# The experts' down projection in eight slices of the model's width in place of four, with the first feed-forward's gate and up taken chunk by chunk

## The chip, the cores and the metric

One core of a Trainium2 chip runs the whole network in one launch. The number that counts is the device time of that launch in microseconds (us). Engines are named by their parts in the profile: PE is TensorE's matmuls, PEld its weight loads, DVE VectorE, ACT ScalarE, POOL GpSimd, SP SyncE (which issues the DMAs). PSUM is the matmuls' accumulator memory, SBUF the memory that all engines read.

## The reference

For 256 tokens of width 1024, in float32:

```python
def expert_choice_moe(h, w_router, w_gate, w_up, w_down):   # 16 experts, 32 tokens each
    aff = softmax(h @ w_router)                              # tokens x experts
    gate, idx = top_k(aff.T, 32)                             # each expert picks its tokens
    xin = h[idx]
    hid = silu(xin @ w_gate) * (xin @ w_up)                  # hidden width 1024
    y = (hid @ w_down) * gate[..., None]                     # back to width 1024
    return zeros_like(h).at[idx].add(y)                      # combine over experts

x = x + expert_choice_moe(rms_norm(x), ...)                  # end of the first block
h = x + 0.5 * (silu(n @ w_g) * (n @ w_u)) @ w_d              # n = rms_norm(x), d_ff 2816
```

Ahead of these lines stands the first block's mixer (dilated attention and a gated recurrence); behind them come two layers with a mixer and a second feed-forward each, and in layer two a first one again. The change touches the experts' down projection (`y` and the combine) and the first feed-forward of the first layer, the last line above.

## The kernel before

Activations lie transposed: `xt` holds x as eight chunks of 128 features by 256 tokens. Weights come from memory once, in a stream of tiles of mostly 1 MiB, [128, 2048] float32. The list `stream` fixes their order; `pump` and `fetch` (L369 to L384) issue the DMAs on SyncE in that order as slots come free: 4 raw slots, and 17 ring slots of 1 MiB (`RING`). The ring also holds `xt`, the hidden values `HT` (two), the normed chunks `norm.x` (two), the partial sums `Pt` (six) and the split pairs. `st["hold"]` is the number of ring slots that stream tiles may not take.

Two kinds of tiles are in the stream. Expert weights go to TensorE as float32 as they are, which the trace shows as two records for each matmul. The others are split (`cut`, L394 to L406) into a high part by ScalarE and a low part by VectorE, and `mm3` (L478 to L481) multiplies them in three matmuls (low by high, high by low, high by high).

The down projection of the experts goes by slices of the model's width, four of 256 columns. In a slice there are 16 y steps, each with one tile: for four experts at a time, two of the eight 128-rows of the hidden width. The four experts stand in the four column groups of TensorE (32 columns each), so that a step is 2 x 4 matmuls. After four steps ScalarE copies the accumulator `y` to SBUF, and TensorE combines it by `SC` (scatter and gate in one matrix) into `moe`. After 16 steps `x` adds `moe` to two chunks of `xt`, and `Norm.split` makes their normed high and low parts without the root of the mean, which is a factor for each token and is multiplied in later (`norm.rb2`).

So the first feed-forward's gate and up can begin before the experts are done. A unit `("u", s, j)` takes hidden chunk j of 22 and the two chunks of x of slice s: 12 matmuls into one PSUM accumulator `gu` (three buffers, tag B). Units of slice 0 are copied to `Pt` by ScalarE, those of slices 1 and 2 added to `Pt` by VectorE. `quarters()` writes the order by hand: slice 0 has y steps alone; in slices 1 to 3 the units of the slice before stand between the y steps, from the fourth step on; of slice 2 five units (`KEEP`) come behind the last y step. The same order places the gate/up tiles `gs` in the stream, two y tiles early (`EARLY`).

Behind that, `first_ffn` takes slice 3's units, ends the norm (`fin1`, `fin2`), and goes through the 22 hidden chunks: unit, `evac` (add to Pt, times norm, silu, product, high and low part), `down` three chunks behind (24 matmuls into four PSUM accumulators).

Each engine works off its own queue in order. The tile framework's scheduler chooses that order from the order of the program text, the dependences, and its own cost estimates; so units and y steps on TensorE need not stand as `quarters()` lists them.

Of the kernel before, what the change touches and what calls it, by code (L numbers as in the profile page):

```python
# [32 lines left out]
NF = 22  # L33
RING, RAW, T1, T2 = 17, 4, 10, 10
WARM = (12, 32)
KEEP, EARLY = 5, 2
# [113 lines left out]
def _prepare(i):  # L150
# [12 lines left out]
    dn = f["w_expert_down"][0].reshape(4, 4, 4, 2, 128, 4, 256)  # L163
    out["wd"] = dn.transpose(5, 0, 2, 4, 3, 1, 6).reshape(4, 4, 4, 128, 2048)
    st = [128 * j for j in range(NF)]
    for l in range(2):
        for n in ("ffn1", "ffn2"):
            ga, up = _pairs(f[n + "_gate_2"][l], st), _pairs(f[n + "_up_2"][l], st)
            both = np.stack([ga, up], axis=3)
            if (n, l) == ("ffn1", 0):  # L170
                q = both.reshape(NF, 128, 4, 2, 2, 128).transpose(2, 1, 3, 0, 4, 5)
                out["f0g"] = q[:, :, :, :20].reshape(4, 128, 2, 5, 1024).transpose(0, 3, 1, 2, 4).reshape(4, 5, 128, 2048)
                out["f0h"] = q[:, :, :, 20:].reshape(4, 128, 1024)
                out["ffn1d0"] = _rows(f["ffn1_down_2"][0])
                continue
# [63 lines left out]
def _body(tc, nc, const, ringp, work, psum, a, out):  # L239
# [66 lines left out]
    def quarters():  # L306


        for q in range(4):
            yield from (("y", 0, q, i) for i in range(4))  # L310
            yield ("sc", 0, q)
        yield ("x", 0)
        for s in range(1, 4):
            n, todo = 0, 22 if s < 3 else 22 - KEEP
            sc = None
            for k in range(16):
                yield ("y", s, k // 4, k % 4)
                while n < todo and n * 13 < (k - 2) * todo:
                    yield ("u", s - 1, n)
                    n += 1  # L320
                if sc:
                    yield sc
                sc = ("sc", s, k // 4) if k % 4 == 3 else None
            while n < todo:
                yield ("u", s - 1, n)
                n += 1
            yield sc
            yield ("x", s)
        yield from (("u", 2, j) for j in range(22 - KEEP, 22))

    order, DS, GS = [], {}, {}
    for op in quarters():
        if op[0] == "y":
            order.append(op[1:])
        elif op[0] == "u" and op[2] % 4 == 0:
            order.insert(len(order) - EARLY, ("gs", op[1], op[2] // 4))
    for o in order:
        if o[0] == "gs":
            GS[o[1:]], = add([a["f0g"][o[1], o[2]] if o[2] < 5 else a["f0h"][o[1]]], 1, 1)
# [3 lines left out]
    for j in range(22):  # L343
        if j % 4 == 0:
            GS[3, j // 4], = add([a["f0g"][3, j // 4] if j < 20 else a["f0h"][3]], 1, 1)
# [919 lines left out]
    def quarter_steps():  # L1265
# [4 lines left out]
        def unit(s, j):  # L1270
            i = GS[s, j // 4]
            n = 4 if j < 20 else 2
            ahead(i)
            wh, wl = (w[:, :512 * n].rearrange("p (c j m o) -> p c j m o", c=2, j=n, m=2) for w in parts[i])
# [9 lines left out]
        for op in quarters():  # L1284
            if op[0] == "y":
                _, s, q, i = op
                pump()
                if i == 0:
                    py[s, q] = pa("y", (128, 256))
                k = DS[s, q, i]  # L1290
                w = raw[k].rearrange("p (k g n) -> p k g n", k=2, g=4)
                for c in range(2):
                    for g in range(4):
                        e = 4 * q + g
                        h = HT[e // 8][:, e % 8].rearrange("p h j s -> p (h j) s")
                        PE.matmul(py[s, q][32 * g:32 * g + 32], lhsT=h[:, 2 * i + c], rhs=w[:, c, g],  # L1296
                                  start=i == 0 and c == 0, stop=i == 3 and c == 1, skip_group_check=True,
                                  tile_position=(0, 32 * g))
                done(k)
                if i == 3:  # L1300
                    ys[s, q] = t1("ys")
# [422 lines left out]
```

## Time and profile before

| what | us |
| --- | --- |
| median of 3 runs | 1580.06 (1580.02 to 1580.49) |
| the profiled execution | 1579.6 |
| its span, first to last instruction | 1577.8 |
| PE busy | 1436.9 (91%) |
| DVE busy | 890.6 (56%) |
| ACT busy | 660.1 (42%) |
| mean DMA rate | 254 GB/s, 400.67 MB |

In the page's forty slices of 39.4 us, the experts are where TensorE's digit falls to 6 and 7 and the DMA's stands at 9: from about 300 to 700 us. The page's chain of the work that ended last gives PE 69% and DMA 23%, of which the gate/up tiles of the experts have 16% and their down tiles (`w<-in_wd`) 6%. A row such as `L1296 PE MATMUL y<-w,hidT 128*32 128x256 f32` is line 1296, TensorE, a matmul that writes tile `y` from `w` and `hidT`, with weights of 128 rows by 32 columns and an output of 128 by 256; `[0.79 <-DMA w<-in_wd]` says that the engine was idle for 0.79 us before it until that DMA landed.

### The profile page before, as it was taken

What the parts mean: (1) busy time and instruction counts of PE and PEld (TensorE: products, weight loads), DVE (VectorE), ACT (ScalarE), POOL (GpSimd) and SP (SyncE); (2) the same over time, 40 slices, a digit from 0 to 9 for tenths busy, and PEclk for the clock granted to TensorE, in tenths of its full rate; (3) what the DMA queues carried; (4) which work ended last, traced back from release to release, by engine and by line L of the source; (5) the groups of instructions that cost most, each with busy time, mean ns of one, the idle gap of its engine ahead of it and who ended that gap; (6) DMA issues with size and microseconds to landing.
All of it is one profiled execution on the core that took longest, in us unless ns stands there. A gap on an engine that the chain in (4) does not pass through costs nothing.

```text
span 1577.8 us, 25243 instructions
## 1 busy us (share of the span) xinstructions
PE 1436.9 (91%) x10552; PEld 1121.4 (71%) x10552; DVE 890.6 (56%) x1628; ACT 660.1 (42%) x1136; POOL 6.1 (0%) x11
## 2 busy tenths in 40 slices
PE   9999986676666789899999999999999999999997
PEld 8987721101112567679999988888888899988886
DVE  7976520000000224469969877675967849877673
ACT  6445220000000341145647665464645637665452
POOL 0000000000000000000000000000000000000000
PEclk9999997766768899999999999999999999999998
DMA  7536799999999889995634635554655634636440
GB/s 297 195 131 225 307 393 421 421 421 421 421 421 421 360 344 351 402 354 184 232 128 163 241 119 220 179 191 156 217 184 187 224 117 173 242 117 221 170 161 27
DMA packets 59442, 400.67 MB, mean 254 GB/s; under 512 B 6592, under 2 KB 9792, under 8 KB 11968
## 3 DMA queue, kind: packets, MB, share of 16 engines
q1 hardware_dynamic: 59184, 398.93, 65.9%
q8 instruction: 82, 1.34, 0.3%
q14 instruction: 32, 0.26, 0.0%
q10 hardware_dynamic: 144, 0.14, 0.0%
HBM read 397.99 MB, written 1.05 MB: 253 GB/s over the span
## 4 chain that ended last, share of the span: by engine, by line
PE 69%; DMA 23%; DVE 5%; ACT 2%; issue 1%; SPq 0%; DVEq 0%; ACTq 0%
DMA w<-in_we 16%; PE gu L486 16%; PE gu L487 8%; PE dn L486 8%; DMA w<-in_wd 6%; PE dn L487 4%; PE gu L479 3%; PE gu L480 2%; PE gu L481 2%; PE y L1296 2%; PE acc L480 2%; PE acc L479 1%; PE acc L481 1%; DVE wl L403 1%; PE dn L479 1%; PE dn L481 1%
## 5 line engine op out<-in xcount | busy, mean ns | idle before, releaser
L403 DVE TENSOR_TENSOR wl<-w,wh 128x1024 fp32r<-128x1024 f32 (+1 forms) x369 | 435.5, 1204 | 92.0 <-ACT wh L402 84.3
L402 ACT ACTIVATE wh<-w 128x1024 fp32r<-128x1024 f32 (+1 forms) x369 | 364.6, 1037 | 47.5 <-PE dn L486 14.9
L486 PE MATMUL gu<-xs,wh 128*128 128x512 f32 x1056 | 371.7, 395 | 0.0
L487 PE MATMUL gu<-xs,wl 128*128 128x256 f32 x1056 | 294.7, 279 | 0.0
L1233 PE MATMUL gu<-w,xin 128*32 128x512 f32 x1024 | 182.3, 806 | 67.8 <-DMA w<-in_we 67.5
L486 PEld LDWEIGHTS gu<-xs,wh 128*128 128x128 f32 x1056 | 197.9, 188 | 45.9
L487 PEld LDWEIGHTS gu<-xs,wl 128*128 128x128 f32 x1056 | 199.2, 189 | 0.2
L486 PE MATMUL dn<-hx,wh 128*128 128x512 f32 x528 | 186.6, 394 | 0.0
L1233 PEld LDWEIGHTS gu<-w,xin 128*32 128x32 f32 x1024 | 26.1, 123 | 199.6 <-DMA w<-in_we 177.8
L1239 DVE TENSOR_TENSOR hid<-sg,gu 64x512 f32<-64x512 f32 x16 | 11.0, 690 | 249.3 <-ACT sg L1238 249.3
L487 PE MATMUL dn<-hx,wl 128*128 128x256 f32 x528 | 147.5, 279 | 0.0
L486 PEld LDWEIGHTS dn<-hx,wh 128*128 128x128 f32 x528 | 99.0, 187 | 23.2
L1296 PE MATMUL y<-w,hidT 128*32 128x256 f32 x1024 | 79.6, 417 | 35.7 <-DMA w<-in_wd 35.7
L479 PE MATMUL gu<-xs,wl 128*128 128x256 f32 x352 | 103.7, 297 | 0.3 <-DVE wl L403 0.3
L481 PE MATMUL gu<-xs,wh 128*128 128x256 f32 x352 | 100.7, 287 | 0.0
L480 PE MATMUL gu<-xs,wh 128*128 128x256 f32 x352 | 100.7, 287 | 0.0
L487 PEld LDWEIGHTS dn<-hx,wl 128*128 128x128 f32 x528 | 99.6, 189 | 0.0
L1238 ACT ACTIVATE sg<-gu 64x512 f32<-64x512 f32 x16 | 9.4, 590 | 209.8 <-PE gu L1233 209.8
L1394 ACT ACTIVATE fl<-gu 128x256 f32<-128x256 f32 x132 | 49.4, 377 | 95.7 <-PE gu L487 95.4
L1395 DVE TENSOR_TENSOR fz<-gu,fl 128x256 f32<-128x256 f32 x132 | 55.2, 419 | 57.3 <-ACT fl L1394 57.1
L1296 PEld LDWEIGHTS y<-w,hidT 128*32 128x32 f32 x1024 | 31.5, 117 | 73.4 <-DMA w<-in_wd 43.9
L479 PEld LDWEIGHTS gu<-xs,wl 128*128 128x128 f32 x352 | 68.5, 196 | 13.2 <-issue 7.7
(397 smaller groups left out, 2489.4 us busy)
## 6 DMA issues: line engine op xcount, KB each, us to landing
w<-in_we SPq DMA_DIRECT2D x128, 1024.0 KB, 19.8
w<-in_wd SPq DMA_DIRECT2D x64, 1024.0 KB, 12.8
w<-in_ffn2gu SPq DMA_DIRECT2D x44, 1024.0 KB, 5.0
w<-in_ffn1d SPq DMA_DIRECT2D x22, 1024.0 KB, 5.3
w<-in_wm SPq DMA_DIRECT2D x22, 1024.0 KB, 4.9
w<-in_ffn2d SPq DMA_DIRECT2D x22, 1024.0 KB, 5.4
w<-in_ffn1gu SPq DMA_DIRECT2D x22, 1024.0 KB, 5.0
w<-in_f0g SPq DMA_DIRECT2D x20, 1024.0 KB, 7.3
```

The costliest lines, as they stand in the source:

```text
L402: hi = S.activation(wh, raw[i][:, a0:a1], AF.Copy)
L403: lo = V.tensor_tensor(wl, raw[i][:, a0:a1], wh.bitcast(F32), op=OP.subtract)
L479: PE.matmul(ps, lhsT=wl, rhs=x[:, 1], start=first, stop=False, skip_group_check=True)
L480: PE.matmul(ps, lhsT=wh, rhs=x[:, 0], start=False, stop=False, skip_group_check=True)
L481: PE.matmul(ps, lhsT=wh, rhs=x[:, 1], start=False, stop=last, skip_group_check=True)
L486: PE.matmul(ps, lhsT=wh, rhs=x, start=first, stop=False, skip_group_check=True)
L487: PE.matmul(ps[:, 0], lhsT=wl, rhs=x[:, 1], start=False, stop=last, skip_group_check=True)
L1233: PE.matmul(pg[32 * g:32 * g + 32], lhsT=xin[k // 4][:, k % 4, 32 * e:32 * e + 32], rhs=w[:, g], start=k == 0, stop=k == 7, skip_group_che ...
L1239: i = V.tensor_tensor(hid, sg, pg[64:128], op=OP.mult)
L1296: PE.matmul(py[s, q][32 * g:32 * g + 32], lhsT=h[:, 2 * i + c], rhs=w[:, c, g], start=i == 0 and c == 0, stop=i == 3 and c == 1, skip_grou ...
L1394: S.activation(zl[:, m], p[m][:, 0], AF.Copy)
L1395: V.tensor_tensor(z[:, m], p[m][:, 1], zl[:, m], op=OP.add)
```

## The change

The down projection goes by eight slices of 128 columns. A slice has eight y steps; a step's tile, again 1 MiB, holds four of the eight 128-rows for four experts, so that a step is 4 x 4 matmuls over 128 columns. Two steps fill an accumulator `y` (128 x 128), which is copied and combined as before, in one matmul of 128 columns by 256 tokens. After eight steps one chunk of `xt` is complete and normed.

A unit takes one chunk of x: six matmuls. There are eight times 22 of them. The units of chunk c stand between the y steps of slice c + 1, spread evenly by `8 * n < NF * (8 * c - 8 + k + 1 - LAG)`, without the gaps at the head of a slice. Gate/up tiles hold eight units (two tiles and one of six units, 0.75 MiB, for each chunk). `hold` falls to 6 after the first slice, where it was 7. Behind the last y step, the last chunk's units are added to `Pt` at once (`gate_up`), `evac` comes two chunks behind the unit and loses the add, and `down` follows six chunks behind the unit.

```diff
-KEEP, EARLY = 5, 2
+LAG, EARLY = 2, 2
...
+    def slices():
+        units = [("u", c, j) for c in range(7) for j in range(NF)]
+        n, sc = 0, None
+        for c in range(8):
+            for k in range(8):
+                yield ("y", c, k // 2, k % 2)
                 if sc:
                     yield sc
+                    if sc[2] == 3:
+                        yield ("x", sc[1])
+                sc = ("sc", c, k // 2) if k % 2 else None
+                while n < len(units) and 8 * n < NF * (8 * c - 8 + k + 1 - LAG):
+                    yield units[n]
+                    n += 1
+        yield sc
+        yield ("x", 7)
+        yield from units[n:]
...
             p = pb("gu")
             for m in range(2):
-                for c in range(2):
-                    mm3(p[:, m], wh[:, c, j % 4, m], wl[:, c, j % 4, m], norm.x[2 * s + c], m == 0 and c == 0,
-                        m == 1 and c == 1)
-            if j % 4 == n - 1:
+                mm3(p[:, m], wh[:, j % 8, m], wl[:, j % 8, m], norm.x[c], m == 0, m == 1)
+            if j % 8 == n - 1:
                 done(i)
...
-                w = raw[k].rearrange("p (k g n) -> p k g n", k=2, g=4)
-                for c in range(2):
+                w = raw[k].rearrange("p (k g n) -> p k g n", k=4, g=4)
+                for c in range(4):
                     for g in range(4):
...
-                    macc[s] = pa("moe")
-                y = ys.pop((s, q))
-                for m in range(2):
-                    PE.matmul(macc[s][:, m], lhsT=y[:, 128 * m:128 * m + 128], rhs=SC[q // 2][:, q % 2],
-                              start=q == 0 and m == 0, stop=q == 3 and m == 1, skip_group_check=True)
+                    macc[s] = pa("moe", (128, 256))
+                PE.matmul(macc[s], lhsT=ys.pop((s, q)), rhs=SC[q // 2][:, q % 2],
+                          start=q == 0, stop=q == 3, skip_group_check=True)
...
-                if s == 0:
-                    st["hold"], st["la"], st["late"] = 7, 1, 0
+                V.tensor_tensor(xt[:, c], macc[c], xt[:, c], op=OP.add)
+                norm.chunk(c)
+                if c == 0:
+                    st["hold"], st["la"], st["late"] = 6, 1, 0
...
+        def gate_up(j):
+            z = Pt[j // 4][:, j % 4]
+            V.tensor_tensor(z, unit(7, j), z, op=OP.add)
+
         def evac(j):
             z = Pt[j // 4][:, j % 4]
-            V.tensor_tensor(z, ps.pop(j), z, op=OP.add)
...
-        for j in range(3):
-            ps[j] = unit(3, j)
+        for j in range(6):
+            gate_up(j)
             if j == 0:
                 norm.fin1(pa)
         norm.fin2()
-        for j in range(3):
+        for j in range(4):
             evac(j)
-        for j in range(3, NF):
-            ps[j] = unit(3, j)
-            evac(j)
-            down(j - 3)
+        for j in range(6, NF):
+            evac(j - 2)
+            gate_up(j)
+            down(j - 6)
         norm.free()
         st["hold"], st["la"], st["late"] = 2, LA[1], LATE[1]
-        for j in range(NF - 3, NF):
+        for j in range(NF - 6, NF):
+            if j < NF - 4:
+                evac(j + 4)
             down(j)
```

The weights are laid out on the host to match (`wd` as 8 x 4 x 2 tiles, `f0g` as 8 x 2, `f0h` as 8).

## Rows read from the trace of the kernel before

**Rows 1.** The windows view (us, busy per engine, granted clock, DMA): three stages.

```profile
473.50:528.00 54.50, 32.85 (x337) 13.66 (x336) 2.53 (x6) 5.32 (x12) 0.00 (x0) 0.81 1.01 420
528.00:704.00 176.00, 158.57 (x1473) 121.18 (x1474) 70.06 (x87) 52.61 (x79) 0.00 (x0) 0.95 0.91 359
704.00:808.00 104.00, 104.00 (x874) 103.69 (x873) 94.73 (x156) 57.47 (x93) 0.21 (x1) 1.00 0.61 213
```

**Rows 2.** The timeline (start us, us, what): first slice's y steps on TensorE.

```profile
511.73 1.07 PE L1296 MATMUL y<-w,hidT 128*32 128x256 f32 x16 [1.41 <-DMA w<-in_wd]
...
529.20 1.03 PE L1296 MATMUL y<-w,hidT 128*32 128x256 f32 x2 [3.12 <-DMA w<-in_wd]
```

**Rows 3.** Timeline of TensorE: one y step, the last y step, the last combine.

```profile
637.49 1.05 PE L1296 MATMUL y<-w,hidT 128*32 128x256 f32 x10 [0.79 <-DMA w<-in_wd]
638.47 0.38 PE L479 MATMUL gu<-xs,wl 128*128 128x256 f32 x1
...
702.38 1.07 PE L1296 MATMUL y<-w,hidT 128*32 128x256 f32 x16
...
704.91 1.03 PE L1309 MATMUL moe<-scat,ys 128*128 128x256 f32 x4
705.59 0.47 PE L479 MATMUL gu<-xs,wl 128*128 128x256 f32 x1
```

**Rows 4.** Waits of SyncE's DMA queue (us, times, longest), 473 to 704 us.

```profile
SPq L374 <- PE y L1296: 83.5, 24, 7.4
```

**Rows 5.** Chain of waits, 570 to 600 us.

```profile
586.84 6.99 DMA w<-in_wd
```

**Rows 6.** Timeline of TensorE: first matmuls of gate/up and down, tail's steady part and end.

```profile
739.45 0.29 PE L479 MATMUL gu<-xs,wl 128*128 128x256 f32 x1
...
740.89 0.28 PE L479 MATMUL dn<-hx,wl 128*128 128x256 f32 x1
...
743.72 0.29 PE L479 MATMUL gu<-xs,wl 128*128 128x256 f32 x1
...
807.75 0.29 PE L479 MATMUL lx<-xs,wl 128*128 128x256 f32 x1
```

**Rows 7.** The page's groups (busy, mean ns | idle before): the y matmuls.

```profile
L1296 PE MATMUL y<-w,hidT 128*32 128x256 f32 x1024 | 79.6, 417 | 35.7 <-DMA w<-in_wd 35.7
```

**Rows 8.** Lines by form: the 128-column float32 matmul.

```profile
L438 PE MATMUL junk<-x,cst 128*128 128x128 f32 x64 | 7.7, 277 | 0.0
```

**Rows 9.** Timeline of TensorE: 128x32 weights over 32 columns.

```profile
52.91 0.71 PE L821 MATMUL lev<-AL,AR 128*32 128x32 f32 x62
53.56 0.39 PE L479 MATMUL aqk<-xs,wl 128*128 128x256 f32 x1
```

**Rows 10.** Timeline of VectorE in the tail.

```profile
741.77 0.68 DVE L1346 TENSOR_TENSOR Pt<-gu,Pt 128x512 f32<-128x512 f32 x1
742.37 0.42 DVE L516 TENSOR_TENSOR hx<-fh,hx 128x256 fp32r<-128x256 f32 x1
...
743.30 2.35 DVE L403 TENSOR_TENSOR wl<-w,wh 128x1024 fp32r<-128x1024 f32 x2
745.57 0.42 DVE L1350 TENSOR_TENSOR fh<-fs,Pt 128x256 f32<-128x256 f32 x1
```

**Rows 11.** Chain of waits, 704 to 726 us.

```profile
724.60 0.47 PE dn L479 x4
```

**Rows 12.** Waits, 528 to 704 us (us, times, longest).

```profile
DVE wl L403 <- ACT wh L402: 59.0, 12, 10.9
...
PEld gu L479 <- DVE wl L403: 2.6, 6, 0.8
...
PEld gu L479 <- DVE Pt L1334: 1.6, 4, 0.4
```

More of the change, by code (lines that the diff above doesn't have):

```diff
@@ L162, in _prepare @@
     out["we"] = gu
[L163 to L164 removed]
+    dn = f["w_expert_down"][0].reshape(4, 4, 2, 4, 128, 8, 128)
+    out["wd"] = dn.transpose(5, 0, 2, 4, 3, 1, 6).reshape(8, 4, 2, 128, 2048)
     st = [128 * j for j in range(NF)]
@@ L302, in _body, with add_gs @@
     GU, DN, WM, WO = {}, {}, {}, {}
[L306 to L320, printed above, removed]
+    def slices():
[4 more added lines that the diff above has]
+                yield ("y", c, k // 2, k % 2)
                 if sc:
                     yield sc
[L323 to L329, printed above, removed]
+                    if sc[2] == 3:
[7 more added lines that the diff above has]
+        yield from units[n:]
     order, DS, GS = [], {}, {}
-    for op in quarters():
+    for op in slices():
         if op[0] == "y":
             order.append(op[1:])
-        elif op[0] == "u" and op[2] % 4 == 0:
-            order.insert(len(order) - EARLY, ("gs", op[1], op[2] // 4))
+        elif op[0] == "u" and op[2] % 8 == 0:
+            order.insert(len(order) - EARLY, ("gs", op[1], op[2] // 8))
+    def add_gs(c, g):
+        GS[c, g], = add([a["f0g"][c, g] if g < 2 else a["f0h"][c]], 1, 1)
     for o in order:
         if o[0] == "gs":
-            GS[o[1:]], = add([a["f0g"][o[1], o[2]] if o[2] < 5 else a["f0h"][o[1]]], 1, 1)
+            add_gs(*o[1:])
         else:
@@ L342, in _body @@
     d0 = []
-    for j in range(22):
-        if j % 4 == 0:
-            GS[3, j // 4], = add([a["f0g"][3, j // 4] if j < 20 else a["f0h"][3]], 1, 1)
+    for j in range(NF):
+        if j % 8 == 0:
+            add_gs(7, j // 8)
         if j >= 3 and (j - 3) % 2 == 0:
@@ L1262, in _body, with slice_steps, unit @@
     rfree(2)
-    def quarter_steps():
+    def slice_steps():
         norm, Pt, py, ys, macc = None, [], {}, {}, {}
-        def unit(s, j):
-            i = GS[s, j // 4]
-            n = 4 if j < 20 else 2
+        def unit(c, j):
+            i = GS[c, j // 8]
+            n = 8 if j < 16 else 6
             ahead(i)
-            wh, wl = (w[:, :512 * n].rearrange("p (c j m o) -> p c j m o", c=2, j=n, m=2) for w in parts[i])
+            wh, wl = (w[:, :256 * n].rearrange("p (j m o) -> p j m o", j=n, m=2) for w in parts[i])
             p = pb("gu")
             for m in range(2):
-                for c in range(2):
-                    mm3(p[:, m], wh[:, c, j % 4, m], wl[:, c, j % 4, m], norm.x[2 * s + c], m == 0 and c == 0,
-                        m == 1 and c == 1)
-            if j % 4 == n - 1:
+                mm3(p[:, m], wh[:, j % 8, m], wl[:, j % 8, m], norm.x[c], m == 0, m == 1)
+            if j % 8 == n - 1:
                 done(i)
             return p
-        for op in quarters():
+        for op in slices():
             if op[0] == "y":
@@ L1295, in quarter_steps @@
                         h = HT[e // 8][:, e % 8].rearrange("p h j s -> p (h j) s")
-                        PE.matmul(py[s, q][32 * g:32 * g + 32], lhsT=h[:, 2 * i + c], rhs=w[:, c, g],
-                                  start=i == 0 and c == 0, stop=i == 3 and c == 1, skip_group_check=True,
+                        PE.matmul(py[s, q][32 * g:32 * g + 32], lhsT=h[:, 4 * i + c], rhs=w[:, c, g],
+                                  start=i == 0 and c == 0, stop=i == 1 and c == 3, skip_group_check=True,
                                   tile_position=(0, 32 * g))
                 done(k)
-                if i == 3:
-                    ys[s, q] = t1("ys")
+                if i == 1:
+                    ys[s, q] = t1("ys")[:, :128]
                     S.activation(ys[s, q], py.pop((s, q)), AF.Copy)
@@ L1338, in first_ffn @@
         st["hold"] = 5
-        norm, Pt, unit = quarter_steps()
+        norm, Pt, unit = slice_steps()
         warm(AF.Silu)
         st["hold"], st["la"], st["late"] = 1, LA[0], LATE[0]
-        ps, hs, acc = {}, {}, []
+        hs, acc = {}, []
+        def gate_up(j):
+            z = Pt[j // 4][:, j % 4]
+            V.tensor_tensor(z, unit(7, j), z, op=OP.add)
         def evac(j):
             z = Pt[j // 4][:, j % 4]
-            V.tensor_tensor(z, ps.pop(j), z, op=OP.add)
             V.tensor_tensor(z, z, norm.rb2, op=OP.mult)
```

24 lines of the change are left out of this document (9 added, 15 removed).

## The prediction

> **What bounds the kernel now.** I read the windows view first. It cuts the touched stretch into three stages [rows 1]: from the first y step to 528 us the transfers are full (420 GB/s, share 1.01) and TensorE waits; from 528 to 704 us both are nearly full and neither wholly (TensorE busy 158.6 of 176, 359 GB/s); from 704 to 808 us TensorE never pauses and VectorE is busy 94.7 of 104. Everything behind 808 us is untouched code, so I let the rest of the span follow the end of this stretch one for one.
>
> 1 MiB at 420 GB/s takes 2.50 us, the unit of all sums below. The timeline shows the first stage at that pace: the sixteenth y step, last of slice 0, starts at 511.7, just after its tile has landed [rows 2]. Back from there by 15 tiles, the tile of the first step has its place in the pace at 511.7 - 37.5 = 474.2. The first gate/up matmul comes only behind 529.2, after two y records of slice 1's fifth step [rows 2]. Until then TensorE has next to nothing to do; a y step is 0.98 us (637.49 to 638.47 [rows 3]).
>
> In the second stage a transfer-only clock would bring the last y tile after 63 y tiles and 16 MiB of gate/up weights: 474.2 + 79 x 2.50 = 671.7. It ran at 702.4 [rows 3]. So 30.7 us were lost over 48 steps, 0.64 us a step. The waits view says how: SyncE's queue stood 83.5 us for slots that a y step had yet to free [rows 4]; then the chain shows the bill, a y tile issued at 586.8 when a slot came free and 7 us in flight while TensorE had nothing left [rows 5]. TensorE bunches gate/up units, tiles that have landed hold their slots meanwhile, the transfers pause, and then TensorE pauses.
>
> In the third stage a unit of gate/up takes 1.44 us and one chunk of the first down projection 2.83 (starts at 739.45, 740.89 and 743.72 [rows 6]). 27 units and 22 downs make 38.9 + 62.3 = 101.2 of the 104.4 us between the end of the last y step (702.38 + 0.98) and the next phase's first matmul at 807.75 [rows 3, 6].
>
> **The change part by part.**
>
> *Slice 0 is half as long.* The first slice is 8 tiles, and chunk 0's units start behind the eleventh y step (LAG of 2). That tile has one gate/up tile ahead of it, so it lands at 474.2 + 11 x 2.50 = 501.7, and units may start at about 502.7 in place of 530. This is the gain: 27 us of TensorE time that is idle now.
>
> *The y steps.* 64 tiles of 1 MiB as before, but each is 16 matmuls over 128 columns in place of 8 over 256; y records go from 1024 [rows 7] to 2048. The array time is equal if the four column groups still run side by side: a group of four records is 0.86/4 = 0.22 us now (0.98 less the start) and should take 0.11 with half the columns. A plain 128-column float32 record costs 7.7/64 = 0.12 us [rows 8], and the trace has a burst with 32-column weights that issues 62 records in 0.65 us, 0.0105 each [rows 9]; four of these are 0.04, well under 0.11, so issue and weight loads hide. I take 0.98 us a step. From the other side, if nothing overlapped, 32 x 0.12 = 3.84 us a step; the burst is the nearer row, being the same tiling.
>
> A rule of the Trainium skill speaks against this. Its page TensorE: Matmul & The Clock Gate, section Back-to-back issue gap, gives about 81 ns per matmul for a sustained stream of load and matmul pairs at 128 columns. By it a step would be an estimated 32 x 0.081 = 2.6 us. The burst of rows 9 at 0.0105 us disagrees with a floor of that size for column-tiled records, so I do not use it for the sum.
>
> *Gate/up units.* 176 half-units of six matmuls, 0.72 us each; the total on TensorE is unchanged. A step of slices 1 to 7 carries 22/8 = 2.75 of them: 1.98 us, with y 0.98 and the combine (32 matmuls as before; four take 705.59 - 704.91 = 0.68 us by records, two records per quarter now, 0.17 a step) 3.13 us. The transfers per step are 1 + 2.75/8 = 1.344 MiB: 3.36 us. SyncE issues the same number (88) and the same bytes.
>
> *The two clocks to the last y step.* Transfers: 63 y tiles and seven chunks of 2.75 MiB: 474.2 + 82.25 x 2.50 = 679.8. TensorE: 502.7 + 53 x 3.13 = 668.6. Transfers end last, by 11, so the two are about as close as in the kernel before and the coupling decides what is lost. The loss per step is bounded by 0 (no bunching) and 0.64 (as now, 36 us over 56 steps). Three things differ: the three unit-free steps at the head of each slice are gone, a unit is half as long, and the slots held back fall from 7 to 6, so of the 17 ring slots six rather than five are left for tiles and split pairs beside the four raw ones. A bunch is still up to one gate/up tile (8 half-units, 5.8 us, as 4 units were). I take 0.38 a step, 21 us: the last y step starts at 701.
>
> *VectorE.* Each half-unit behind chunk 0 is added to Pt separately: 154 adds in place of 66, 88 more at 0.60 us (741.77 to 742.37 [rows 10]), 53 us. About 127 fall into the y stage, whose VectorE is busy 70 of 176 now [rows 1]: per step 2.75 x 0.60 + 0.344 x 2.27 for the splits (two cuts, 743.30 to 745.57 [rows 10]) + 0.15 for the norm = 2.6 of 3.36 us. It fits, so I cost it at nothing there; its cover is that slack, and without it a stall of three accumulators follows (rival below). ScalarE's copies of y are twice as many over half the columns, and 22 Pt copies stay. GpSimd's queue is not touched.
>
> *The tail.* Left behind the last y step are 5 half-units of chunk 6 and 22 of chunk 7, 27 x 0.72 = 19.4 us, and the downs, 62.3: with the norm's small matmuls 84. The first down waits for the whole norm; now it starts at 724.6 [rows 11], 19 us behind the combine, and these 19 us are just what the 27 half-units cover, because their adds no longer stand behind the norm. VectorE: what it does in 704 to 808 now (94.7) less the splits of 2.75 MiB (6.2) is 88.5. Tail between 84 and 92; I take 88, VectorE's number, against 104.4.
>
> Sum: 701 + 1 + 88 = 790 against 807.75, 18 us less. The profiled execution took 1579.6 (span 1577.8), 0.5 under the median of 1580.06; the forecast is on the median: **1562 us**.
>
> **The rivals.**
>
> A. *As forecast*, 1562 (1552 to 1571 with the tail's bounds and a loss of 0.25 to 0.5 a step). Chance 0.48.
>
> B. *The bunching stays.* If slots, not unit size, make the loss, it is 0.64 a step again: the last y step at 716, end 805, 3 us less: 1577 (1573 to 1581). For it: SyncE's 83.5 us of waits for y [rows 4]. Against: one slot more and evener units. Chance 0.17.
>
> C. *Even spreading removes nearly all of it*: 8 us lost, tail 84: end 773, 35 less: 1545. For it: TensorE still has 0.23 us a step to spare. Against: no stretch of the second stage shows it. Chance 0.15.
>
> D. *Slower: VectorE stops TensorE through the three gate/up accumulators.* VectorE works in order, and now stands 59.0 us in 12 waits at the head of a split for ScalarE's half, 4.9 us each; TensorE lost only 2.6 + 1.6 us by it [rows 12], since three accumulators were 4.3 us of work. With half-units, two free ones cover 1.44. A wait of 4.9 and the add behind it (0.6) then cost 5.5 - 1.44 = 4.1. If 10 of the 24 gate/up tiles catch it, TensorE's clock gains 41, less the 12 it has to spare over 53 steps: 29 late, end at 819: 1591. It decides from about seven tiles (7 x 4.1 - 12 = 17). Against: the waits now are mostly VectorE idling with nothing else to do. Chance 0.15.
>
> E. *The column groups stop overlapping*: 3.84 a step, TensorE needs 5.99 a step, the last y step at 820, 1680. Against: [rows 9]. Chance 0.05.
>
> By the skill's 81 ns, E would give an estimated 502.7 + 53 x 4.74 + 88 = 842, about 1614.
>
> **How the numbers follow.** 0.2% (3.2 us) is about what a measurement can tell from no change. A and C are faster, as is half of B: 0.48 + 0.15 + 0.09 = 0.72; the other half of B is no change: 0.08; D and E slower: 0.20. The range 1541 to 1584 holds A, B and nearly all of C, and leaves out E and most of D, with C's far end about 0.2. The likeliest case's own range is 1552 to 1571.
>
> **What would show it.** The first gate/up matmul at about 503 us; y records 2048, with a step of 32 near 1.0 us; last y step near 701, with SyncE's waits for y well under 83 us; 154 adds into Pt with hardly any TensorE wait for VectorE before the last y step; the next phase's first matmul near 790, VectorE full in the tail. It is wrong if a y step takes over 1.4 us, if TensorE's waits for Pt adds exceed 15 us (D), or if the last y step stays behind 710 (B).

## The result, and the profile after

The changed kernel takes **1591.59 us** (1590.80 to 1593.75 in 4 runs) where the one before takes 1580.28 beside it: a ratio of 1.0072, 95% interval 1.0055 to 1.0089. It is slower by 11 us (the profiled executions' spans are 1589.8 and 1577.8). The forecast was 1562, 30 us less, with a range that ends at 1584.

The windows view of the changed kernel, cut where the first gate/up matmul, the last y step and the next phase begin, answers to [rows 1]. The columns are the same: length, busy time of TensorE, its weight loads, VectorE, ScalarE and GpSimd, granted clock, DMA share, GB/s.

```profile
473.50:516.60 43.10, 27.46 (x476) 19.26 (x476) 2.14 (x5) 5.03 (x12) 0.00 (x0) 0.76 1.01 420
516.60:724.70 208.10, 187.19 (x2514) 161.13 (x2514) 135.47 (x185) 60.46 (x100) 0.00 (x0) 0.98 0.88 340
724.70:820.00 95.30, 89.10 (x729) 87.71 (x718) 88.47 (x148) 50.01 (x86) 0.00 (x0) 0.95 0.57 203
```

The first stage is 13.5 us shorter than before (gate/up began at 530.2), the second 35 longer (173 before, from that matmul to the last y step), the third 9 shorter (104.4 before). Net, the next phase starts 12.2 us later. In the middle stage the transfers run at 340 GB/s, below before's 359, while TensorE still pauses for 21 us: neither is full.

The start, on ScalarE's timeline of the changed kernel (start, length, what; the bracket is the idle time ahead):

```profile
494.32 0.42 ACT L545 ACTIVATE ss<-x 128x256 f32<-128x256 f32 x1 [1.25 <-DVE x L1310]
501.11 0.28 ACT L1299 ACTIVATE ys<-y 128x128 f32<-128x128 f32 x1 [6.38 <-PE y L1293]
508.57 0.28 ACT L1299 ACTIVATE ys<-y 128x128 f32<-128x128 f32 x1 [7.18 <-PE y L1293]
513.75 0.28 ACT L1299 ACTIVATE ys<-y 128x128 f32<-128x128 f32 x1 [4.91 <-PE y L1293]
513.93 0.50 ACT L532 ACTIVATE xs<-x,vec 128x256 fp32r<-128x256 f32 x1
514.33 1.99 ACT L401 ACTIVATE wh<-w 128x1024 fp32r<-128x1024 f32 x2
```

Chunk 0 of x is summed by 494.3 and its first gate/up tile has landed at 496.6, but the normed chunk (`xs`) and the tile's high part (`wh`) stand in ScalarE's queue behind three copies of y, each of which waits 5 to 7 us for its y steps. ScalarE is idle nearly all of these 19 us. The first gate/up matmul starts at 516.68.

The middle, in the chain of waits of the changed kernel (start, length, what), the place where a gate/up tile begins:

```profile
583.04 1.05 PE y L1293 x32
584.14 0.15 issue
584.29 1.06 ACT wh L401
585.37 1.24 DVE wl L402
586.60 0.14 issue
586.74 0.36 PE gu L478
```

The copy of y between them is on ScalarE's timeline:

```profile
584.11 0.28 ACT L1299 ACTIVATE ys<-y 128x128 f32<-128x128 f32 x1 [6.15 <-PE y L1293]
584.29 1.99 ACT L401 ACTIVATE wh<-w 128x1024 fp32r<-128x1024 f32 x2
```

A y step ends, ScalarE copies it, then splits the next gate/up tile, then VectorE makes the low part, and only then TensorE goes on with that tile. The transfer is not what is late: this tile had landed at 565.9, 18 us before its split began, and each of the first twenty gate/up tiles of the stage lay for 10 to 18 us. The waits view counts what TensorE lost, over 473 to 720 us (us, times, longest):

```profile
PE gu L478 <- DVE wl L402: 18.4, 16, 2.9
PE y L1293 <- DMA w<-in_wd: 13.6, 11, 3.8
PEld gu L478 <- DVE Pt L1325: 3.4, 17, 0.2
...
SPq L373 <- PE y L1293: 100.0, 27, 9.1
SPq L373 <- DVE wl L402: 81.1, 19, 13.7
```

Sixteen waits of a matmul for a low part, where before there were two, 0.3 us in all (weight loads had the 2.6 of [rows 12]). SyncE's queue waits longer for y steps than in [rows 4], and longer for splits (a raw slot comes free when its tile is split; 64.3 before).

The end of the stretch, on TensorE's timeline of the changed kernel, answers to [rows 3, 6, 11]:

```profile
723.86 1.08 PE L1293 MATMUL y<-w,hidT 128*32 128x128 f32 x32
...
739.91 0.69 PE L569 MATMUL rbT<-cst,rt 128*128 128x128 f32 x2 [2.06 <-DVE rt L473]
743.87 1.01 PE L478 MATMUL dn<-hx,wl 128*128 128x256 f32 x3 [3.28 <-ACT hx L514]
...
819.97 0.29 PE L478 MATMUL lx<-xs,wl 128*128 128x256 f32 x1
```

The y matmuls on the page, against [rows 7]:

```profile
L1293 PE MATMUL y<-w,hidT 128*32 128x128 f32 x2048 | 79.3, 292 | 13.6 <-DMA w<-in_wd 13.6
```

Twice the records, half the columns, the same busy time (79.6 before). A step's 32 records take 1.08 us, 0.034 each. For these records, with 32-column weights in four column groups, the trace disagrees with the 81 ns that the Trainium skill (TensorE: Matmul & The Clock Gate, section Back-to-back issue gap) gives for each matmul in a stream of load and matmul pairs at 128 columns.

### The profile page after: what moved, and what is told of

It is laid out like the page before. It is cut to its first block, busy times and chain, and to the rows that moved or that the text cites. A ratio compares the mean times of both kernels' runs of the same rounds, so it can differ in the third digit from the quotient of the medians.

```text
span 1589.8 us, 27418 instructions
## 1 busy us (share of the span) xinstructions
PE 1445.0 (91%) x11576; PEld 1150.3 (72%) x11576; DVE 949.6 (60%) x1716; ACT 660.6 (42%) x1152; POOL 6.1 (0%) x11
## 4 chain that ended last, share of the span: by engine, by line
PE 70%; DMA 18%; DVE 8%; ACT 3%; issue 1%; DVEq 0%; SPq 0%; ACTq 0%
PE gu L485 15%; DMA w<-in_we 15%; PE gu L486 8%; PE dn L485 8%; PE dn L486 4%; PE y L1293 3%; DVE wl L402 3%; PE gu L478 3%; DMA w<-in_wd 3%; PE gu L479 2%; PE gu L480 2%; ACT wh L401 2%; PE acc L479 2%; PE acc L478 1%; PE acc L480 1%; PE gu L1232 1%
## 5 line engine op out<-in xcount | busy, mean ns | idle before, releaser
L401 ACT ACTIVATE wh<-w 128x1024 fp32r<-128x1024 f32 (+2 forms) x369 | 364.7, 1037 | 26.2 <-PE dn L485 14.9
L478 PE MATMUL gu<-xs,wl 128*128 128x256 f32 x352 | 107.1, 304 | 18.6 <-DVE wl L402 18.4
L485 PEld LDWEIGHTS dn<-hx,wh 128*128 128x128 f32 x528 | 99.0, 188 | 23.1
L1325 DVE TENSOR_TENSOR Pt<-gu,Pt 128x512 f32<-128x512 f32 x132 | 89.9, 690 | 41.1 <-PE gu L480 39.5
L1293 PE MATMUL y<-w,hidT 128*32 128x128 f32 x2048 | 79.3, 292 | 13.6 <-DMA w<-in_wd 13.6
L1390 ACT ACTIVATE fl<-gu 128x256 f32<-128x256 f32 x132 | 49.4, 376 | 95.7 <-PE gu L486 95.4
```

The costliest lines, as they stand in the source:

```text
L401: hi = S.activation(wh, raw[i][:, a0:a1], AF.Copy)
L478: PE.matmul(ps, lhsT=wl, rhs=x[:, 1], start=first, stop=False, skip_group_check=True)
L485: PE.matmul(ps, lhsT=wh, rhs=x, start=first, stop=False, skip_group_check=True)
L1293: PE.matmul(py[s, q][32 * g:32 * g + 32], lhsT=h[:, 4 * i + c], rhs=w[:, c, g], start=i == 0 and c == 0, stop=i == 1 and c == 3, skip_grou ...
L1325: V.tensor_tensor(Pt[j // 4][:, j % 4], p, Pt[j // 4][:, j % 4], op=OP.add)
L1390: S.activation(zl[:, m], p[m][:, 0], AF.Copy)
```

## The experiments

All are edits of the changed kernel, so the yardstick is 1591.59; ratios are to the kernel before. Times of stages are from each run's own trace: "first unit" is the first gate/up matmul (after: 516.7), "last y" the start of the last y record (724.7), "end" the next phase's first matmul (820.0). Behind it all traces have the same 769.8 to 771.0 us.

**Which part costs: the split's place, the adds, the half-units, the slices.** e_split2 fetches each gate/up tile one y step earlier and splits it two earlier.

```diff
-LAG, EARLY = 2, 2
+LAG, EARLY, SOON = 2, 3, 2
...
+            elif op[0] == "u" and op[2] % 8 == 0:
+                cuts.setdefault(max(ny - SOON, 0), []).append(GS[op[1], op[2] // 8])
...
                 pump()
+                for k in cuts.get(ny, []):
+                    split(k)
```

> The changed kernel with each gate/up tile's split put two y steps ahead of the tile's first unit in the program (and the tile itself one y tile earlier in the stream); nothing is computed more or less. Theory S (the split is asked for only when its first unit is due, its ScalarE half stands behind a y copy and its VectorE half behind Pt adds, and TensorE stands at the first unit: about 4 of each slice's 32 us): TensorE's waits for the split nearly go, a slice takes 28 to 29 us, the last y step comes at 695 to 705 in place of 724, about 1570 us. Theory V (VectorE's 88 more adds set the pace): its work is the same, so 1588 to 1593. Theory P (TensorE's own time grew, by twice as many changes between y and units): 1588 to 1593.

1584.40, ratio 1.0026 (1.0016 to 1.0036): 7 us off. TensorE's waits for the low part fall from 18.4 to 10.3, last y 715.3, where theory S wanted 695 to 705. The late split costs, but it is not all.

e_noadd leaves the adds of chunks 1 to 6 out.

```diff
-                else:
+                elif c == 6 and j >= 17:
                     V.tensor_tensor(Pt[j // 4][:, j % 4], p, Pt[j // 4][:, j % 4], op=OP.add)
```

> The changed kernel without the adds into Pt of chunks 1 to 6 ahead of the last y step (it leaves these parts of gate and up out of the sum). Theory V: VectorE loses about 76 us of work in the y stage, so the stage shrinks by 20 us or more, to about 1570 us. Theory S: the VectorE half of a split no longer stands behind adds, but its ScalarE half still stands behind the y copy and the split is still asked for late: 3 to 10 us, 1581 to 1588. Theory P: no change in the y stage, 1589 to 1593.

1586.53, ratio 1.0038 (1.0027 to 1.0050): with VectorE's work in the middle stage cut from 135 to 53 us, only 5 us come off, and 14.8 us of TensorE's waits for low parts stay. The adds are the smaller part of it.

e_pairs keeps the eight slices and takes units of two chunks, as before; e_single keeps four slices and takes units of one chunk.

```diff
-        units = [("u", c, j) for c in range(7) for j in range(NF)]
+        units = [("u", s, j) for s in range(3) for j in range(NF)]      # e_pairs
...
-            for k in range(8):
-                yield ("y", c, k // 2, k % 2)
+            for k in range(16):                                         # e_single
+                yield ("y", c, k // 4, k % 4)
```

> One part alone: the down projection in eight slices of 128 columns, but gate/up units of two chunks (12 matmuls, 66 adds) as before the change, which can begin only behind the second slice. If the 128-column y steps cost time by themselves: above 1585 us. If the halved units do (S, V and P all say so): within 5 us of the kernel before, 1577 to 1584.

> The other part alone: the down projection in four slices of 256 columns as before, but gate/up units of one chunk, spread evenly, and the changed tail; units begin only behind the first slice of 16 y steps. S, V and P: the stage pays for the halved units without the earlier start: 1592 to 1605 us. If the halved units were free: 1575 to 1582.

e_pairs 1586.73, ratio 1.0037 (1.0023 to 1.0050); e_single 1608.38, ratio 1.0169 (1.0147 to 1.0191). Their first units start at 530.6 and 532.3, as before. Neither isolates one part: both spread the units evenly, and e_single has the changed tail too. By its own bounds e_pairs (above 1585) speaks for y steps that cost something. Its trace does not show that: a y record occupies 0.0335 us there (a step 1.07), but TensorE waits 12.4 us for low parts, which the kernel before hardly does (0.3). e_single loses otherwise than the changed kernel: of its 28 us over the kernel before, 18 lie between the first unit and the last y record (190.9 against 172.9), with 21 us of waits for y tiles, and 8 behind it (112.9 against 104.7). That the whole change costs less than e_single goes with its early start; no run shows that it is the only reason.

**The start.** x_norm takes the two ring slots of the normed chunks at the start of the stage, by a one-column write, so that `xs` need not wait for y tiles to leave them. x_pre0 does that, and takes two pairs of parts (used in turn by all gate/up tiles up to chunk 6) and the six slots of `Pt` ahead as well. x_pre2 is x_pre0 with e_split2's earlier fetch and split; x_pre2t adds to x_pre2 that the last chunk's adds come behind the norm's root.

```diff
-        norm, Pt, py, ys, macc = None, [], {}, {}, {}
+        norm, Pt, py, ys, macc = Norm(vc("ffn1n", 0, 8)), [], {}, {}, {}
+        for h in norm.x.half:
+            V.tensor_copy(h[:, 0, 0, 0:1], xt[:, 0, 0:1])
...
+        pairs, turn = [tuple(ralloc([128, 2048], F32R, n) for n in ("wh", "wl")) for _ in range(2)], [0]   # x_pre0, x_pre2
...
-LAG, EARLY = 2, 2
+LAG, EARLY, SOON = 2, 3, 2                    # x_pre2 (x_pre0: 2, 2, 0)
...
+            if j:
+                behind(add, st["gate"])       # x_pre2t
```

> The changed kernel with the two ring slots of the normed chunks taken ahead of the first y step (by a one-column write), where they were taken when the first slice was done. Theory R (slots: transfers that stand further down the program take every ring slot as it comes free, so the normed chunks, the split pairs and Pt get theirs only when a y step frees one, and their ScalarE halves stand behind that step's copy): chunk 0's high part comes at 494 in place of 513.9, but the first split pair still has to wait for a slot, so the first gate/up matmul moves only from 516.7 to 507 to 513, and the total to 1582 to 1590 us. Rival S (only the place of the split in the program): the first gate/up matmul at about 503, the rest as in the changed kernel, 1577 to 1581 us.

> The changed kernel with all that the stage keeps taken from the ring ahead of the first units: the normed chunks, two split pairs that are used in turn, and the six Pt tiles; two ring slots and the four raw ones are left for tiles. The split stands where it stood in the program. Theory R: first gate/up matmul at 502 to 507, few waits for splits, last y step at 695 to 705 (724 in the changed kernel), 1565 to 1575 us. Rival S: only the start gets better; the waits inside the slices stay, 1577 to 1585 us. Rival Q (fewer tiles in flight starve TensorE of y tiles): 1590 us or more.

> As the run with all kept slots taken ahead, and each split asked for two y steps before its first unit. R alone: within 3 us of that run, either way. S beside R: 3 to 12 us better than it, 1558 to 1570 us.

> As the run before it, and in the tail the adds of the last chunk's units and the splits further ahead stand behind the root of the mean on VectorE, which in the changed kernel took 6.4 us for eight small operations with an add between any two of them, while TensorE stood 6 us until the first down. If that order costs the tail its 6 to 7 us over the forecast of 88: 4 to 7 us better than the run before it. If the tail is bound by VectorE's sum of work: within 2 us of it.

x_norm: 1593.41, ratio 1.0078 (1.0061 to 1.0095), nothing gained. Its ScalarE timeline:

```profile
495.41 0.51 ACT L532 ACTIVATE xs<-x,vec 128x256 fp32r<-128x256 f32 x1 [1.25 <-DVE x L1310]
...
513.85 0.28 ACT L1301 ACTIVATE ys<-y 128x128 f32<-128x128 f32 x1 [4.74 <-PE y L1295]
514.02 2.00 ACT L401 ACTIVATE wh<-w 128x1024 fp32r<-128x1024 f32 x2
```

`xs` moved by 18.5 us, `wh` by 0.3: the split's own slots hold it there, and first unit stays at 517.4.

x_pre0: 1579.32, ratio 0.9991 (0.9981 to 1.0002). First unit at 499.3, 17 us earlier; the end moves by 13, because the middle stage became 5 longer: though it has its own pairs of parts, TensorE still waits 23.1 us for low parts (473 to 720 us). x_pre2: 1611.29, ratio 1.0197 (1.0182 to 1.0212), and x_pre2t 1613.18, ratio 1.0206 (1.0191 to 1.0221). The same early start, and then a middle stage of 244 us. TensorE's waits in x_pre2, 498 to 742 us:

```profile
PE gu L479 <- DVE wl L402: 35.1, 19, 3.7
```

Of the 17 ring slots two are left for tiles in flight there, with the four raw ones six in all. At one such wait the gate/up tile lands at 602.3, ScalarE begins its high part at 603.06, and TensorE stands from 601.85 to 605.50: the tile itself is late. I read it so that slots help at the start, where they are missing, and cost later, where tiles in flight lack them. x_pre2t says that the adds ahead of the root are not what the tail waits for: its tail is no shorter than x_pre2's (98.3 us against 97.9).

**Bunching, and the tail.** x_bunch puts all the units of a gate/up tile behind one y step, the opposite of the change's even spread. x_bunchpre is x_bunch with x_pre0's slots. a_norb leaves out the multiplication by the norm's factor for all hidden chunks but the first, 12.6 us of VectorE in the tail. x_bpool is x_bunchpre with half of that multiplication on GpSimd.

```diff
-                    yield units[n]
-                    n += 1
+                    m = min(8, NF - n % NF)               # x_bunch, x_bunchpre, x_bpool
+                    yield from units[n:n + m]
+                    n += m
...
-            V.tensor_tensor(z, z, norm.rb2, op=OP.mult)
+            if j == 0:                                    # a_norb
+                V.tensor_tensor(z, z, norm.rb2, op=OP.mult)
...
+            V.tensor_tensor(z[:, 0], z[:, 0], norm.rb, op=OP.mult)    # x_bpool
+            G.tensor_tensor(z[:, 1], z[:, 1], norm.rb, op=OP.mult)
```

> The changed kernel with the units of a whole gate/up tile (8, 8 and 6) behind one y step each, where two or three stood behind every y step; so there are three changes from y to units in a slice, not seven or eight, and all 154 units come ahead of the last y step (5 more, 3.5 us). Theory P (TensorE's own time grew: 135 ns for a gate/up record and 0.56 us for a combine, against 119 ns within a run, by the changes between kinds): gate/up records fall to 122 to 128 ns, the stage by 6 to 12 us, total 1578 to 1586 us. Theory R (slots alone): the splits still wait for a slot, 1588 to 1594 us.

> The bunched units together with all kept slots taken ahead. If P and R are two costs that add: 8 to 14 us better than the run with the slots alone (1579.3), 1565 to 1572 us, faster than the kernel before. If the one took the place of the other: 1576 to 1582 us.

> The changed kernel without the factor of the norm on hidden chunks 1 to 21 in the tail (it leaves that factor out; chunk 0 keeps it, so that the downs still wait for the root). VectorE loses 21 x 0.60 = 12.6 us of work behind the root. If VectorE's sum of work bounds the tail: 6 to 12 us less, 1579 to 1586 us. If the root's chain or TensorE bounds it: within 3 us of 1591.

> The bunched units with all kept slots taken ahead, and in the tail the up half of that factor on GpSimd, which is idle, in place of VectorE (22 x 0.27 us off VectorE). If VectorE bounds the tail and GpSimd keeps pace: 3 to 6 us better than without, 1560 to 1569 us. If GpSimd's instruction takes over 2 us or slows VectorE: no better or worse.

x_bunch: 1583.16, ratio 1.0013 (1.0001 to 1.0025), 8 us off the changed kernel. Its waits of TensorE, 517 to 718 us:

```profile
PE y L1294 <- DMA w<-in_wd: 9.5, 12, 1.8
...
PE gu L479 <- DVE wl L403: 0.9, 4, 0.3
```

The waits for low parts are gone: while TensorE does a bunch, the next split has time. In their place y steps wait 9.5 us for their tiles (1.0 in the changed kernel from its first unit on), so TensorE's pauses fall from 20.8 to 15.5 only; the other 3 us of the stage are TensorE's own time (184.0 against 187.2). With the changed kernel's slots, even spreading, which the forecast took for a gain, was a loss of 8; v_first and v_firstb below show that this does not hold with other slots. x_bunchpre, 1583.29 (1.0014; 1.0001 to 1.0026): the early start adds nothing to that, since the slots taken ahead bring the waits for low parts back (20.6 us).

a_norb: 1591.94, ratio 1.0071 (1.0054 to 1.0087). Its tail:

```profile
729.60:822.80 93.20, 87.83 (x727) 86.67 (x718) 76.67 (x127) 49.51 (x86) 0.00 (x0) 0.96 0.59 206
```

VectorE 12 us freer, the tail 2 us shorter: it is not VectorE's sum that bounds it. x_bpool, 1586.11 (1.0038; 1.0023 to 1.0053), is 3 us above x_bunchpre, but it did not relieve VectorE. VectorE's multiplication of one half took 0.81 us beside GpSimd's 0.95 for the other, where that of both halves took 0.685 in x_bunchpre; VectorE's busy time in the tail rose from 85.1 to 90.0 us. So this run says nothing on what the tail waits for.

**Do the two costs add?** v_first takes ahead only what the first unit needs: the normed chunks' slots and one pair of parts for the first tile, which then goes back to the ring; the two slots are held free from the eleventh expert on. v_firstb adds the bunching, v_firstbs a split one y step earlier to that, v_bs has those two without the slots.

```diff
-        parts[i] = (ralloc([128, 2048], F32R, f"wh{i}"), ralloc([128, 2048], F32R, f"wl{i}"))
+        parts[i] = st.pop("pair", None) or (ralloc([128, 2048], F32R, f"wh{i}"), ralloc([128, 2048], F32R, f"wl{i}"))
...
+        if e == 11:
+            st["hold"] += 2
...
+        pair = tuple(ralloc([128, 2048], F32R, n) for n in ("wh", "wl"))
+        for w in pair:
+            V.tensor_copy(w[:, 0:1], xt[:, 0, 0:1])
+        st["pair"] = pair
```

> The changed kernel, with only the slots of the normed chunks and of one pair of high and low parts taken ahead, at the eleventh expert (x_pre0 took two pairs and the four slots of Pt as well). Start theory (the first gate/up matmul waits for slots, and nothing that is taken for it is missed later): that matmul at 500 to 505 us, last y step 710 to 714, total 1577 to 1582. Rival (what x_pre0 gained came from its two alternating pairs of parts, not from the early start): the matmul early all the same, but the last y step at 718 to 724 and a total of 1584 to 1591.

> v_first, and the eight units of a gate/up tile together behind one y step, as in x_bunch. If the two costs add (start 12 to 17 us, units together 8): last y step at 700 to 706, total 1568 to 1575, below the kernel before. Rival (both draw on the same slots, and an early start only makes the later tiles wait): total 1580 to 1585, as x_bunch and x_bunchpre.

> v_firstb, and each tile is split one y step earlier (e_split2 did that to the changed kernel and took 7 us off). Split theory (TensorE still stands for the parts at a tile's first unit): 2 to 5 us below v_firstb, and the waits of gate/up matmuls for the low part below 8 us. Rival (after putting the units together no split wait on the path is left, and the earlier split only holds a pair of slots longer): within 2 us of v_firstb or up to 6 us above it.

> The changed kernel with the units together and the split one y step earlier, and no slots taken ahead. Start theory: the first gate/up matmul stays at 515 to 520, and the total at 1577 to 1582, above v_firstbs by 8 to 15 us. Rival (the start is worth nothing once the stage's pace is better, since y steps wait for the transfers): within 3 us of v_firstbs.

v_first: **1569.46** (1568.45 to 1571.13), ratio 0.9931 (0.9914 to 0.9947), faster than both kernels. v_firstb 1584.32 (1.0032; 1.0017 to 1.0046), v_firstbs 1583.06 (1.0021; 1.0006 to 1.0036), v_bs 1582.29 (1.0017; 1.0005 to 1.0029): with the units together the early start is worth nothing, so these two do not add. More than that: with v_first's slots, putting the units together costs 15 us, where it gained 8 with the changed kernel's. v_first is over 7 us better than its start theory allowed, and the start alone does not explain it: the first unit comes 17.2 us earlier, the last y record 20.6 (704.1), the end 20.5. Its waits for low parts are 3.0 us.

**Which slots.** v_pair is v_first with the pair alone taken ahead, and not the normed chunks. It also leaves `hold` at 5 when the stage begins, which v_first lowers to 1 for its four slots, so fewer ring slots are open to tiles in its first slice. v_firsts is v_first with e_split2's edit.

```diff
-        norm, Pt, py, ys, macc = Norm(vc("ffn1n", 0, 8)), [], {}, {}, {}
-        for h in norm.x.half:
-            V.tensor_copy(h[:, 0, 0, 0:1], xt[:, 0, 0:1])
+        norm, Pt, py, ys, macc = None, [], {}, {}, {}             # v_pair
...
-LAG, EARLY = 2, 2
+LAG, EARLY, SOON = 2, 3, 2                                        # v_firsts
```

> v_first without the normed chunks' slots: only one pair of high and low parts is taken ahead. x_norm showed the chunks' slots alone to give nothing (first gate/up matmul at 517.4, total 1593). Theory that both are needed: the normed chunk waits behind the evictions as in the changed kernel, the first gate/up matmul stays at 513 to 518, and the total at 1585 to 1592. Rival (the pair does all of it): the matmul at 500 to 505 and the total within 3 us of v_first's 1569.

> v_first, and each gate/up tile fetched one and split two y steps earlier, as e_split2 did to the changed kernel for 7 us. If the split's lateness is gone in v_first (gate/up matmuls wait 3.0 us for the low part in it): within 2 us of 1569, or up to 8 us above it because the parts hold their slots longer and y tiles land later. Rival (some lateness is left at each tile's first unit): 1563 to 1567.

v_pair: **1571.06** (1568.62 to 1577.42), ratio 0.9950 (0.9932 to 0.9967). With one pair of slots taken ahead, 20.5 of the 30 us that were missing are back: in the traces the first unit comes 8.3 us earlier and the middle stage is 13.4 shorter (194.7 against 208.1). The total is as the rival said, the first unit between the two. Its windows, its ScalarE at the start and in one slice, and its waits of TensorE and SyncE, 473 to 703 us:

```profile
475.00:508.30 33.30, 19.77 (x390) 14.05 (x388) 3.27 (x4) 4.58 (x10) 0.00 (x0) 0.85 1.01 420
508.30:703.00 194.70, 181.07 (x2596) 158.41 (x2598) 132.57 (x183) 60.57 (x101) 0.00 (x0) 1.00 0.95 376
703.00:798.40 95.40, 88.70 (x728) 87.55 (x721) 88.34 (x149) 51.05 (x86) 0.00 (x0) 0.96 0.61 219
```

```profile
497.36 2.00 ACT L401 ACTIVATE wh<-w 128x1024 fp32r<-128x1024 f32 x2 [1.92 <-DMA w<-in_f0g]
501.80 0.28 ACT L1306 ACTIVATE ys<-y 128x128 f32<-128x128 f32 x1 [2.44 <-PE y L1300]
501.97 0.50 ACT L532 ACTIVATE xs<-x,vec 128x256 fp32r<-128x256 f32 x1
...
577.51 3.46 ACT L401 ACTIVATE wh<-w 128x1024 fp32r<-128x1024 f32 x4
```

```profile
PE gu L478 <- DVE wl L402: 3.3, 6, 0.7
...
SPq L373 <- PE y L1300: 82.1, 28, 5.2
...
SPq L373 <- DVE wl L402: 37.6, 14, 9.1
```

The first split follows its tile's landing (497.36) in place of the third copy of y, and the first unit starts at 508.4, behind a y step whose tile landed at 507.4. The transfers of the first stage run at 420 GB/s all the same. And in the slices ScalarE splits two tiles in one go (577.51, four halves), one of them ahead of its need. That leaves 3.3 us of waits for low parts, halves SyncE's wait for splits, and gives 376 GB/s. A slice takes 29.2 us (577.4 to 606.6), where the changed kernel takes 32.0 (584.1 to 616.1). v_firsts, 1582.60 (1.0010; 0.9997 to 1.0022), has the early start as well (498.2) but 14.9 us of waits for low parts: asking for the split earlier still undoes what v_first gained.

## Why the prediction was wrong

By the traces, the 30.0 us between the end forecast (790) and the one measured (819.97) are 14.0 at the start, 8.9 in the middle and 7.1 in the tail.

**The step that failed first: "units may start at about 502.7".** It asked only for the tile and the chunk, and both were there by 497. It left out that `xs`, `wh` and `wl` each need a ring slot that y tiles held, and that on an engine that works in order a split which waits for a slot is put behind copies that wait for y. Shown: x_norm frees `xs` and nothing moves; v_pair frees the pair and the first unit comes at 508.4, v_first frees both and it comes at 499.5. This step accounts for 14.0 of the 30 us.

**The sizes on TensorE: 3.13 us a step.** From the starts of consecutive records between the first unit and the last y step (waits taken off), a gate/up matmul occupies 0.135 us, a y step 1.11 and a combining record 0.281, against 0.12, 0.98 and 0.17: 25 us more in all (118.5 + 55.1 + 13.5 for 876, 1589 and 48 records). The same count in the same stretch of the kernel before gives 0.131, 1.14 and 0.277. So these are not costs of the change but of that stage; I had taken them from the steady tail and from one step and one combine [rows 3, 6]. For the combine the prediction's own rows spoke otherwise: 0.12 us for a float32 record of 128 columns [rows 8] makes an estimated 0.24 for 256, not 0.17. With 0.131, 1.14 and 0.277 a step is 2.16 + 1.14 + 0.28 = 3.58, above the transfers' 3.36. TensorE, not the transfers, was the longer clock, and had nothing to spare for a wait.

About 4 of the 25 us are the granted clock, and they hang on the waits. The windows view of the changed kernel, in the middle stage and in the tail:

```profile
565.70:569.10 3.40, 3.40 (x18) 3.40 (x18) 1.91 (x4) 0.00 (x0) 0.00 (x0) 0.51 1.00 414
739.80:750.10 10.30, 6.27 (x26) 5.56 (x26) 10.24 (x22) 6.97 (x16) 0.00 (x0) 0.50 0.00 0
```

The clock was at half, 1.2 GHz, in three stretches of the middle stage, each behind a wait for a low part: from 565.7 (a wait of 2.90 us), from 664.7 (2.85) and from 685.2 us (1.26). A gate/up record with another one behind it occupied 0.213 us there against 0.126 at the full clock, which makes the estimated 4 us for 44 records. v_pair, with short waits, had the full clock from 505.8 us to the end of the stage.

**The loss, 21 us**, was right as a sum by luck (20.8 us of TensorE's pauses): it came from the splits, 18.4 us in 16 waits, where the forecast saw late y tiles, and these cost 1.0 from the first unit on. SyncE's waits for y, which were to fall well under 83 us, rose to 100. That the split of a tile must be done by the end of the tile before it was in none of its steps. Whether inside the slices a split is late for want of slots or by its place in ScalarE's queue is not shown: x_pre0 with its own pairs still waits 23.1 us, e_split2 with an earlier place 10.3. v_pair has 13.6 us of pauses and its last y step starts at 702.23, next to the 701 forecast: a shorter loss and a full clock paid for a later start and dearer steps.

**The tail, 88 us by VectorE's number.** VectorE's sum was right (88.5 forecast, 88.47 measured), but that did not set the tail, as a_norb shows. The tail is 95 because TensorE is busy for 89.1, where the forecast had 84, and stands 6.2: 5.3 for the norm's factor, in the gaps ahead of `rbT` and `dn`, and 0.9 for a split. Some 3 of the 5 us more are again the clock (the second row above): behind these gaps the 24 `dn` records from 743.87 to 750.1 take 6.2 us at half the clock, where at 0.12 each they would take 2.9. It is the same in v_pair (95.4), which with 702.23 + 96 us for the last step and the tail ends at 798.4, and with it at 1571.

**Right:** y steps of half the columns cost nothing on TensorE (1.11 us a step in the stage, 1.14 before); so do their 2048 weight loads of 32 columns; the adds fit, TensorE waited 3.4 us for them; E did not come. **Rivals:** D named the right time, 1591, and the right sign, by luck. It had TensorE stop for accumulators that wait for their adds; those waits were 3.4 us, far below its own sign of 15, and without the adds (e_noadd) only 5 us come off. TensorE's waits were for the low parts of the next tile, which no rival had. B was right that slots matter, and its sign came (last y step behind 710), but the loss was not late y tiles, and more bunching helped the changed kernel (x_bunch). C, 8 us of loss from even spreading, came in no run: the least was 12.9 (e_split2).

**What stays open:** why the one pair, taken ahead, leaves every later slice with its splits two in one go. That it does is in the traces of v_pair and v_first, once in each slice; their edits leave every split at its tile's first unit in the program. That the ring's order of slots carries it on from slice to slice is argued only, and with it the cause of 13 of v_pair's 20 us. v_firsts and v_firstb show how easily it is lost. The 6 us of e_pairs are not explained to the end either.

## What to carry to other kernels

When work is moved earlier, list for its first instruction every buffer slot that it takes, not only its data, and what stands ahead of it in each engine's queue: here one pair of slots brought the first unit 8 us forward, and the kernel gained 20, most of it for a reason that stays open, while a version that took twelve slots gained 12. Take durations from the stage they are used in, as means over its records, since a steady stretch elsewhere was 13% too cheap (3.13 against 3.58), enough to name the wrong bound. Spreading work evenly takes away the long stretches in which the next tile gets ready; before doing so, see who prepares the next tile and when. But do not make a rule of either order: putting the units together gained 8 us with one set of slots and lost 15 with another.

## What the runs showed of the hardware

In the changed kernel TensorE waited for tile after tile from 473.5 to 497.5 us (busy 14.2 of 24.0). Then the granted clock was 0.50 (1.2 GHz) to 514.5 us, and a y step of 32 records took 1.94 us there (506.56 on TensorE's timeline) against 1.08 at the full clock later. Three waits of the middle stage were followed by the half clock too, and so cost more than their own length.

Between kinds of matmuls TensorE loses time that no wait shows: at the full clock of the changed kernel's middle stage, a gate/up record with another one behind it occupies 0.126 us by its neighbours' starts (784 records), one with a y step behind it 0.209 (48 records).

VectorE's multiplication was slower beside GpSimd's: in x_bpool it took 0.81 us for 256 columns where GpSimd had the other 256, in x_bunchpre 0.685 for all 512.
